# Hybrid decoder trunk: side work issued ahead of the weight parts in each half chunk, four output columns by turns, and a later rope stage

## The chip, the cores and the metric

One Trainium2 chip, one of its cores. The metric is the device time of one execution in microseconds (us). Three runs of the kernel before gave 1641.02, 1641.28 and 1642.7 us; the median is 1641.28 us.

## What is computed

Two layers over a sequence of 256 tokens of width 1024, batch 1, all in float32. Cut to what matters:

```
for l in range(2):
    x = x + 0.5 * swiglu(rms_norm(x, ffn1_norm[l]), ffn1_w_gu[l], ffn1_w_down[l])
    h = rms_norm(x, mix_norm[l])
    z = h @ w_in[l]           # q_a, k_a, v_a, q_b, f_b, i_b, og_b, gate_a, gate_b
    y_a = dilated_attention(rope(q_a), rope(k_a), v_a) @ w_att_branch[l]     # 3 groups, 4 heads
    o_b = rms_norm(hgrn2_recurrence(q_b, f_b, i_b, lb[l]), hgrn_head_norm[l])  # 8 heads
    y_b = (o_b * silu(og_b)) @ w_hgrn_branch[l]
    x = x + (sigmoid(gate_a) * y_a + sigmoid(gate_b) * y_b) @ w_mix_out[l]
    x = x + cross_attention(rms_norm(x, xattn_norm[l]), rms_norm(mem, mem_norm[l]),
                            xattn_wq[l], xattn_wkv[l], xattn_wo[l])          # 4 heads of 256
    x = x + 0.5 * swiglu(rms_norm(x, ffn2_norm[l]), ffn2_w_gu[l], ffn2_w_down[l])
return rms_norm(x, final_norm)
```

## The kernel before, in words

**Weights.** All weights come through one stream of 4288 blocks of 128 x 128, in the order in which they are used. A chunk is 16 blocks (1 MB, one DMA on the SyncE queue, three buffers `raw`), a half chunk is 8. For precision every weight is split in two: `whi` is the block rounded to the matmul's type (a cast on ScalarE, L104, 128 x 1024 elements for a half chunk), `wlo` is the rest (a subtraction on VectorE, L110). Activations are split in the same way, high part by ScalarE (L277 or L287), low part by VectorE (L280 or L288). One block is two matmuls: L323 multiplies `whi` with both parts of the activation (512 columns), L324 multiplies `wlo` with the high part (256 columns). Where the tokens are the output's rows (`tm`), it is L297 to L299.

**The stream's clock.** `take` hands out blocks. At the first block of half chunk i it calls `prep(i + 3, i + 2)`, which issues `whi` for half chunk i + 3 and `wlo` for i + 2 (five and four buffers), and the load of the chunk two further on. Then it calls `on_half`, which is `tick`. `tick` runs what was deferred to this half chunk and takes one step of one piece of side work. All engines execute in the order of issue.

**Side work.** `defer(n, f)` runs f n half chunks later. `side(generator, period)` adds a generator; each `yield` ends a step. Side work is the norm statistics (`Norm.steps`; of the memory once, with `keep="mem"`, after `mem_stats` has added its squares, L374 on ScalarE and L376 on VectorE, between the half chunks of the first feed-forward), the rope tables and bounds (`setup`), the recurrence (`hgrn`: steps of matmuls L645 and VectorE work L651 to L661; its output matmuls are L692 and L694) and one attention generator per head (`attention`: scores L739 and L743, softmax, transposes L765 to L768, value products L777 and L779).

**A group of matmuls.** `fm` takes a pair buffer of PSUM (there are three; `bank` has two) and multiplies two columns of weights, 16 blocks for an inner size of 1024. The `evac` that it is given runs behind the last matmul. In most stages that is `add_halves`: ScalarE copies one half (L344), and half a chunk later VectorE adds the other (L347), after which the stage's own work follows: in the feed-forward L510 (times the norm), L511 (Silu on ScalarE), and a half chunk later L518 and the split L277 and L280; in the mixer's merged gate L917, L919, L277 and L280. `fm_beside` does the same for four columns by turns in two pair buffers, and runs both `evac`s at the end.

**Residual updates.** `mm_resid` runs an output product column pair by column pair; `Resid.take` then adds both halves to x (L434 on VectorE, twice), forms the next operand's parts (L287 on ScalarE, L288 on VectorE) and adds squares for the next norm (L374 and L376). None of this is deferred.

**The mixer's order** is written out: eight recurrence groups, then values, output gates and gates by turns with the twelve `query_key` groups (three to a head). In `query_key`, `stage1` (half a chunk after the group's end) copies halves on ScalarE (L878, L879) and multiplies on GpSimd (L880); `stage2`, one half chunk later, does L884 and L885 on VectorE; one half chunk after the last group's `stage2` the head's attention begins. What is left then runs in `drain`. Next come the merged gate (eight groups of 12 blocks) and the output product `w_mix_out`.

**In the cross-attention** each head's product of probabilities and values (L293 to L295) goes to a `bank`, and is split by L277 and L280.

Of the kernel before, what the change touches and what calls it, by code (L numbers as in the profile page):

```python
# [12 lines left out]
OP = mybir.AluOpType  # L13
# [4 lines left out]
D = 1024  # L18
P = 128
# [27 lines left out]
class Stream:  # L47
# [65 lines left out]
    def take(self, descs):  # L113

        n = len(self.order)
        i, o = divmod(n, HALF)
        assert o + len(descs) <= HALF
        self.order.extend(descs)
        if o == 0:
            self.prep(i + 3, i + 2)  # L120
            self.on_half()
            self.hi.pop(i - 1, None)
            self.lo.pop(i - 1, None)
        s = slice(o * P, (o + len(descs)) * P)
        return self.hi[i][:, s], self.lo[i][:, s]


def build(tc, a, nchunks):
# [237 lines left out]
    class Norm:  # L366
# [25 lines left out]
        def steps(self, keep=None):  # L392
            st = bank()
            for i in range(2):
                nc.tensor.matmul(st[:, i:i + 1], self.acc[:, i * P:(i + 1) * P], ones[:, :1],
                                 start=True, stop=True)
            ms = tiny.tile([P, 2], F32, name="ms")
            nc.vector.tensor_scalar(ms, st[:, :2], 1.0 / D, EPS, op0=OP.mult, op1=OP.add)
            pool = tiny if keep is None else consts
            self.r = pool.tile([P, 2], F32, name="rstd" + (keep or ""))  # L400
            nc.gpsimd.tensor_tensor(self.r, ms, mhalf[:, :2], op=OP.pow)
            dg = tmp()
            for i in range(2):
                nc.vector.tensor_scalar(dg[:, i * P:(i + 1) * P], ident, self.r[:, i:i + 1], None, op0=OP.mult)
            yield
            yield
            b = bank()
            nc.tensor.matmul(b[:, :T], ones, dg, start=True, stop=True)
            self.bc = (tiny if keep is None else consts).tile([P, T], F32, name="bc" + (keep or ""))
            nc.scalar.copy(self.bc, b[:, :T])  # L410
# [29 lines left out]
    class Last:  # L440
# [32 lines left out]
        def finish(self, g):  # L473
            st = pair()
            for i in range(2):
                s = slice(i * P, (i + 1) * P)
                nc.tensor.matmul(st[:, i:i + 1], self.acc[:, s], ones[:, :1], start=True, stop=False)
                nc.tensor.matmul(st[:, i:i + 1], self.sq[:, s], ones[:, :1], start=False, stop=True)
            ms = tiny.tile([P, 2], F32, name="ms")
            r = tiny.tile([P, 2], F32, name="rstd")  # L480
            nc.vector.tensor_scalar(ms, st[:, :2], 1.0 / D, EPS, op0=OP.mult, op1=OP.add)
            nc.gpsimd.tensor_tensor(r, ms, mhalf[:, :2], op=OP.pow)
            self.turn(KD - 1, g)
            for i in range(2):
                o, y = self.o[i], a["y"][i * P:(i + 1) * P]
                nc.vector.tensor_scalar(o[:, :512], o[:, :512], r[:, i:i + 1], None, op0=OP.mult)
                nc.scalar.activation(o[:, 512:], self.b[i], AF.Copy, scale=r[:, i:i + 1])
                nc.sync.dma_start(y[:, :512], o[:, :512])
                (nc.sync, nc.scalar)[i].dma_start(y[:, 512:], o[:, 512:])

    def mm_resid(name, l, act, K, res):
        n = 2 if K == KD else 1
        for j in range(0, KD, n):
            fm([(name, l, (j + i) * P, act, K) for i in range(n)],
               lambda left, right, j=j: res.take(j, left, right))

# [238 lines left out]
    def attention(l, h, qk, v, out):  # L735
# [21 lines left out]
        nc.vector.tensor_scalar(s0[:, :384], s0[:, :384], den[:, 0:1], None, op0=OP.mult)  # L757
        nc.vector.tensor_scalar(s1[:, :768], s1[:, :768], den[:, 1:2], None, op0=OP.mult)
        yield
        yield  # L760
        b0, b1 = bank(), pair()
        p0, p1 = slot(), slot()
        for g in range(NG):
# [26 lines left out]
    def mixer(l, res, nxt):  # L790
# [76 lines left out]
        def query_key(u):  # L867
            hd, g = divmod(u, NG)
            if g == 0:
                qks[hd] = Row()  # L870
            row = qks[hd]

            def evac(left, right):
                d, t = row.two(2 * g), join()
                r = two(t)

                def stage1():
                    nc.scalar.copy(r[:64], d[64:])  # L878
                    nc.scalar.copy(r[64:], d[:64])  # L879
                    nc.gpsimd.tensor_tensor(r, r, both(sb), op=OP.mult)  # L880
                    defer(1, stage2)

                def stage2():
                    nc.vector.tensor_tensor(d, d, both(cb), op=OP.mult)  # L884
                    nc.vector.tensor_tensor(d, d, r, op=OP.add)  # L885
                    if g == NG - 1:
                        qk = [(row(2 * i), row(2 * i + 1)) for i in range(NG)]
                        defer(1, lambda: side(attention(l, hd, qk, v, aout), 2))
                add_halves(d, left, right, stage1)
            c = g * 512 + hd * P  # L890
            fm([("w_in", l, CQ + c, h, KD), ("w_in", l, CK + c, h, KD)], evac)
# [29 lines left out]
                add_halves(two(t), left, right, stage1, last)  # L921
            fm([("w_att_branch", l, j * P, aout, AH), ("w_hgrn_branch", l, j * P, hout, HH)], evac)
        r = nxt()
        mm_resid("w_mix_out", l, mg, KD, r)
        return r


# [33 lines left out]
    def xattn(l, res, hm, nxt):  # L961
# [30 lines left out]
        drain()  # L992
        o = Act()
        for hd in range(XH):
            b = bank()
            for d in range(2):
                o0 = (2 * (hd % 2) + d) * P
                for c in range(2):
# [114 lines left out]
```

## Time and profile before

| | |
|---|---|
| median of three runs | 1641.28 us |
| lowest and highest | 1641.02 and 1642.7 us |
| the profiled execution's own time | 1640.77 us |
| its span (first to last instruction) | 1639.0 us |
| mean granted clock of TensorE | 0.998 |
| instructions | 26419 |
| HBM read | 286.18 MB |

The span is the time between the first and the last instruction that the profiler saw; 1.77 us lie around it. PE is TensorE's matmuls and PEld its weight loads, DVE is VectorE, ACT ScalarE, POOL GpSimd, SP SyncE. Matmuls are pipelined and their ends are modelled: TensorE is called busy in time in which a matmul is only drawn out, so waits on it are read from starts as well. In a row, the bracket at the end is the engine's idle time before the instruction and what ended it. L numbers are lines of the kernel.

### The profile page before, as it was taken

The numbers are of one execution on the slowest core, as the hardware profiler recorded it, in microseconds if no ns is written. First come the engines' busy times: TensorE is split into PE (matmuls) and PEld (weight loads), VectorE is DVE, ScalarE is ACT, GpSimd is POOL, SyncE is SP. The second block draws the span as 40 slices with busy tenths as digits, with TensorE's granted clock in tenths as the row PEclk, the third lists the DMA queues.
The fourth block names the chain that finished last, engine by engine and source line by source line (L and its number), as shares of the span: only waits on it lengthen the run. The fifth ranks groups of instructions, "written<-read, shape, count | busy, mean of one in ns | idle before, by whom it ended". The sixth has DMA issues, their size and how long they took to land.

```text
span 1639.0 us, 26419 instructions
## 1 busy us (share of the span) xinstructions
PE 1618.5 (99%) x10818; PEld 1414.8 (86%) x10818; DVE 1240.8 (76%) x1804; ACT 925.7 (56%) x1381; POOL 63.0 (4%) x46
## 2 busy tenths in 40 slices
PE   9999999999999999999999999999999999999998
PEld 7888888888888888888888888888888888888887
DVE  7887687767868868877677776777788787688764
ACT  6665454656565656655456655546565656466542
POOL 0000000102100000000000000001111000000000
PEclk9999999999999999999999999999999999999999
DMA  8555554434445534555555564544334454355552
GB/s 303 183 181 211 199 182 180 155 130 154 154 154 180 197 137 171 190 190 196 184 185 197 182 223 176 191 172 150 144 133 159 174 180 179 129 206 180 193 191 79
DMA packets 41593, 288.94 MB, mean 176 GB/s; under 512 B 4864, under 2 KB 4992, under 8 KB 7424
## 3 DMA queue, kind: packets, MB, share of 16 engines
q1 hardware_dynamic: 41040, 286.67, 49.0%
q8 instruction: 85, 1.39, 0.3%
q10 hardware_dynamic: 432, 0.59, 0.1%
q14 instruction: 36, 0.29, 0.1%
HBM read 286.18 MB, written 1.05 MB: 175 GB/s over the span
## 4 chain that ended last, share of the span: by engine, by line
PE 90%; DVE 6%; ACT 2%; issue 1%; DMA 0%; POOLq 0%; POOL 0%; ACTq 0%; DVEq 0%
PE pair L323 49%; PE pair L324 25%; PE pair L297 3%; PE pair L298 3%; PE pair L299 3%; DVE wlo L110 2%; PE bank L645 1%; DVE join L347 1%; DVE slot L280 1%; PE bank L777 1%; PE pair L336 1%; DVE join L917 1%; PE pair L743 0%; PE bank L293 0%; PE bank L294 0%
## 5 line engine op out<-in xcount | busy, mean ns | idle before, releaser
L323 PE MATMUL pair<-slot,whi 128*128 128x512 f32 x3808 | 1337.4, 395 | 4.8 <-DVE slot L280 2.5
L324 PE MATMUL pair<-slot,wlo 128*128 128x256 f32 x3808 | 1065.9, 280 | 0.0
L323 PEld LDWEIGHTS pair<-slot,whi 128*128 128x128 f32 x3808 | 713.4, 187 | 167.4 <-DVE slot L347 3.1
L324 PEld LDWEIGHTS pair<-slot,wlo 128*128 128x128 f32 x3808 | 719.2, 189 | 0.6
L110 DVE TENSOR_TENSOR wlo<-raw,whi 128x1024 fp32r<-128x1024 f32 x532 | 640.1, 1221 | 43.2 <-ACT whi L104 42.9
L104 ACT CAST whi<-raw 128x1024 fp32r<-128x1024 f32 x532 | 546.7, 1046 | 15.5 <-PE pair L299 6.1
L344 ACT COPY join<-pair 128x512 f32<-128x512 f32 x136 | 79.6, 586 | 181.8 <-PE pair L324 181.7
L347 DVE TENSOR_TENSOR join<-pair,join 128x512 f32<-128x512 f32 x136 | 93.7, 690 | 107.1 <-ACT join L344 107.0
L287 ACT ACTIVATE slot<-x,vecs 128x256 fp32r<-128x256 f32 x64 | 30.9, 506 | 133.2 <-DVE x L434 132.0
L297 PE MATMUL pair<-whi,slot 128*128 128x512 f32 x224 | 89.2, 398 | 0.0
L299 PE MATMUL pair<-whi,slot 128*128 128x512 f32 x224 | 87.4, 390 | 0.0
L298 PE MATMUL pair<-wlo,slot 128*128 128x512 f32 x224 | 87.4, 390 | 0.0
L344 ACT COPY slot<-pair 128x512 f32<-128x512 f32 x48 | 28.1, 586 | 102.7 <-PE pair L324 102.7
L277 ACT CAST slot<-join 128x256 fp32r<-128x256 f32 (+1 forms) x120 | 51.7, 435 | 50.8 <-DVE join L919 26.0
L434 DVE SCALAR_TENSOR_TENSOR x<-pair,x 128x256 f32<-128x256 f32 (+1 forms) x80 | 42.5, 531 | 49.2 <-PE pair L324 47.7
L511 ACT ACTIVATE tmp<-join 128x256 f32<-128x256 f32 x88 | 36.4, 417 | 52.5 <-DVE join L510 52.4
L510 DVE TENSOR_TENSOR join<-join,bc 128x512 f32<-128x512 f32 x88 | 60.5, 692 | 5.1 <-ACT bc L410 2.4
L880 POOL TENSOR_TENSOR join<-join,sinb 128x512 f32<-128x512 f32 x24 | 42.1, 1753 | 421.7 <-ACT join L879 392.8
L280 DVE TENSOR_TENSOR slot<-join,slot 128x256 fp32r<-128x256 f32 (+1 forms) x120 | 54.0, 455 | 2.8 <-ACT slot L277 2.8
L347 DVE TENSOR_TENSOR slot<-pair,slot 128x512 f32<-128x512 f32 x48 | 33.1, 689 | 27.5 <-ACT slot L344 27.4
L288 DVE SCALAR_TENSOR_TENSOR slot<-x,vecs,slot 128x256 fp32r<-128x256 f32 x64 | 29.6, 484 | 27.0 <-ACT slot L287 27.0
L299 PEld LDWEIGHTS pair<-whi,slot 128*128 128x128 f32 x224 | 42.0, 188 | 9.0
(184 smaller groups left out, 1029.9 us busy)
## 6 DMA issues: line engine op xcount, KB each, us to landing
raw<-w SPq DMA_DIRECT2D x266, 1024.0 KB, 4.8
slot<-mem SPq DMA_DIRECT2D x6, 512.0 KB, 6.7
raw<-w SPq DMA_DIRECT2D x3, 512.0 KB, 7.8
y<-slot SPq DMA_DIRECT2D x3, 256.0 KB, 2.3
cst<-cst SPq DMA_DIRECT2D x1, 721.0 KB, 10.2
x<-x SPq DMA_DIRECT2D x2, 256.0 KB, 4.3
x<-x SPq DMA_DIRECT2D x1, 512.0 KB, 7.0
raw<-w ACTq DMA_DIRECT2D x1, 256.0 KB, 5.1
```

What stands on the lines that cost most here:

```text
L104: nc.scalar.copy(self.hi[i], r)
L110: nc.vector.tensor_tensor(self.lo[i], r, self.hi[i].bitcast(F32), op=OP.subtract)
L277: nc.scalar.copy(h, src)
L280: nc.vector.tensor_tensor(l, src, h.bitcast(F32), op=OP.subtract)
L297: nc.tensor.matmul(out, ah, wh, start=first, stop=False)
L298: nc.tensor.matmul(out, ah, wl, start=False, stop=False)
L299: nc.tensor.matmul(out, al, wh, start=False, stop=last)
L323: nc.tensor.matmul(whole[:, i * 512:(i + 1) * 512], wh, act.parts(k), start=k == 0, stop=False)
L324: nc.tensor.matmul(whole[:, i * 512:i * 512 + T], wl, act.hi(k), start=False, stop=k == K - 1)
L344: nc.scalar.copy(d, right)
L347: nc.vector.tensor_tensor(d, left, d, op=OP.add)
L510: nc.vector.tensor_tensor(two(t), two(t), both(n.bc), op=OP.mult)
```

## The change

It has six parts. In `take`, `on_half` comes ahead of `prep` (but for the very first half chunk). The memory's norm yields once more ahead of its second matmul. The last norm's four matmuls are put in another order and two PSUM banks. The mixer's output product does its first four columns by turns, with both residual updates at the end. In the mixer, rope's second stage and the attention behind it come two half chunks later instead of one, each, and the attention yields once less after its softmax. In the cross-attention, heads 2 and 3 use pair buffers.

```
 def take(self, descs):
         if o == 0:
+            if i == 0:
+                self.prep(i + 3, i + 2)
+            self.on_half()
             self.prep(i + 3, i + 2)
-            self.on_half()
...
 Norm.steps:
             yield
             yield
+            if keep:
+                yield
             b = bank()
...
 Last.finish:
             for i in range(2):
-                s = slice(i * P, (i + 1) * P)
-                nc.tensor.matmul(st[:, i:i + 1], self.acc[:, s], ones[:, :1], start=True, stop=False)
-                nc.tensor.matmul(st[:, i:i + 1], self.sq[:, s], ones[:, :1], start=False, stop=True)
+                nc.tensor.matmul(st[:, i * 512:i * 512 + 1], self.acc[:, i * P:(i + 1) * P], ones[:, :1],
+                                 start=True, stop=False)
+            for i in range(2):
+                nc.tensor.matmul(st[:, i * 512:i * 512 + 1], self.sq[:, i * P:(i + 1) * P], ones[:, :1],
+                                 start=False, stop=True)
...
-    def mm_resid(name, l, act, K, res):
+    def mm_resid(name, l, act, K, res, turns=False):
         n = 2 if K == KD else 1
-        for j in range(0, KD, n):
+        first = 0
+        if turns:
+            first = 4
+            fm_beside([(name, l, j * P, act, K) for j in range(4)],
+                      [lambda left, right, j=j: res.take(j, left, right) for j in (0, 2)])
+        for j in range(first, KD, n):
...
 attention, after the softmax:
         yield
-        yield
         b0, b1 = bank(), pair()
...
 query_key, stage1 and stage2:
-                    defer(1, stage2)
+                    defer(2, stage2)
...
-                        defer(1, lambda: side(attention(l, hd, qk, v, aout), 2))
+                        defer(2, lambda: side(attention(l, hd, qk, v, aout), 2))
...
 mixer:
-        mm_resid("w_mix_out", l, mg, KD, r)
+        mm_resid("w_mix_out", l, mg, KD, r, True)
...
 xattn:
         for hd in range(XH):
-            b = bank()
+            b = bank() if hd < 2 else pair()[:, :512]
```

## Rows read from the trace of the kernel before

**Rows 1.** The page: busy time of each engine with its share of the span and its instructions, and the loads of weight chunks (number, KB each, median us from issue to landing).
```profile
PE 1618.5 (99%) x10818; PEld 1414.8 (86%) x10818; DVE 1240.8 (76%) x1804; ACT 925.7 (56%) x1381; POOL 63.0 (4%) x46
...
raw<-w SPq DMA_DIRECT2D x266, 1024.0 KB, 4.8
```
**Rows 2.** Busy time by window, of the L323 matmuls alone (one to a block), in a stretch of the first feed-forward. Columns: window, its length, PE busy (instructions), PEld busy (instructions), granted clock, DMA share, GB/s.
```profile
43.96:99.43 55.47, 55.47 (x161) 29.81 (x160) 1.00 0.50 177
```
**Rows 3.** The waits of TensorE's matmuls: engine and line, whom it waited for, us in total, times, longest.
```profile
PE pair L323 <- DVE slot L280: 2.5, 2, 1.6
PE pair L323 <- DVE slot L347: 2.3, 2, 1.2
PE bank L293 <- DVE slot L280: 1.6, 2, 0.8
PE bank L739 <- DVE slot L885: 1.5, 2, 0.8
...
PE bank L408 <- DVE tmp L404: 1.0, 1, 1.0
```
**Rows 4.** The timeline of TensorE in the mixer of layer 0: start, us from the first start to the last end, engine, line, operation, names, shapes, number of instructions merged, idle time before.
```profile
266.48 0.39 PE L298 MATMUL pair<-wlo,slot 128*128 128x512 f32 x1
...
303.67 0.60 PE L739 MATMUL bank<-slot 128*128 128x128 f32 x4
305.03 0.49 PE L739 MATMUL bank<-slot 128*128 128x128 f32 x2 [0.75 <-DVE slot L885]
...
361.03 0.83 PE L739 MATMUL bank<-slot 128*128 128x128 f32 x6
361.69 1.46 PE L743 MATMUL pair<-slot 128*128 128x256 f32 x6
362.80 0.58 PE L323 MATMUL pair<-slot,whi 128*128 128x512 f32 x1
...
406.45 1.46 PE L743 MATMUL pair<-slot 128*128 128x256 f32 x6
...
409.08 0.50 PE L323 MATMUL pair<-slot,whi 128*128 128x512 f32 x1 [1.17 <-DVE slot L347]
...
488.29 0.40 PE L323 MATMUL pair<-slot,whi 128*128 128x512 f32 x1
```
**Rows 5.** The groups of instructions of the whole span: the subtraction that makes `wlo` and the cast that makes `whi` (busy us, mean ns of one, idle time of the engine before them and what ended it).
```profile
L110 DVE TENSOR_TENSOR wlo<-raw,whi 128x1024 fp32r<-128x1024 f32 x532 | 640.1, 1221 | 43.2 <-ACT whi L104 42.9
L104 ACT CAST whi<-raw 128x1024 fp32r<-128x1024 f32 x532 | 546.7, 1046 | 15.5 <-PE pair L299 6.1 <-ACT whi L104 3.6 <-DVE wlo L110 1.7
```
**Rows 6.** The timeline of VectorE over most of one cycle of two half chunks in the first feed-forward of layer 0.
```profile
79.36 0.69 DVE L347 TENSOR_TENSOR join<-pair,join 128x512 f32<-128x512 f32 x1
80.08 0.69 DVE L510 TENSOR_TENSOR join<-join,bc 128x512 f32<-128x512 f32 x1
81.56 0.42 DVE L376 TENSOR_TENSOR tmp<-tmp 128x256 f32<-128x256 f32 x1 [0.79 <-ACT tmp L374]
81.91 1.22 DVE L110 TENSOR_TENSOR wlo<-raw,whi 128x1024 fp32r<-128x1024 f32 x1
83.04 0.42 DVE L518 TENSOR_TENSOR join<-tmp,join 128x256 f32<-128x256 f32 x1
```
**Rows 7.** The timeline of ScalarE in the same cycle.
```profile
77.44 0.59 ACT L344 COPY join<-pair 128x512 f32<-128x512 f32 x1
...
83.49 0.41 ACT L277 CAST slot<-join 128x256 fp32r<-128x256 f32 x1 [1.02 <-DVE join L518]
83.92 1.28 ACT L547 ACT_TABLE_LOAD   x1
```
**Rows 8.** The timeline of VectorE at the recurrence's first step with L645 in layer 0.
```profile
256.20 2.36 DVE L110 TENSOR_TENSOR wlo<-raw,whi 128x1024 fp32r<-128x1024 f32 x2 [3.23 <-ACT whi L104]
260.16 0.69 DVE L347 TENSOR_TENSOR slot<-pair,slot 128x512 f32<-128x512 f32 x1 [1.60 <-ACT slot L344]
...
265.49 0.43 DVE L661 COPY_PREDICATED tmp<-cpm,bank 128x128 f32<-128x128 uint32 x1
```
**Rows 9.** The timeline of ScalarE and VectorE at the start of the merged gate in layer 0.
```profile
481.62 0.58 ACT L344 COPY join<-pair 128x512 f32<-128x512 f32 x1
...
483.07 0.69 DVE L347 TENSOR_TENSOR join<-pair,join 128x512 f32<-128x512 f32 x1
...
484.52 0.42 DVE L919 TENSOR_TENSOR join<-join 128x256 f32<-128x256 f32 x1
...
484.98 0.41 ACT L277 CAST slot<-join 128x256 fp32r<-128x256 f32 x1 [1.84 <-DVE join L919]
```
**Rows 10.** The timeline of VectorE in the mixer's output product of layer 0: the residual updates of the first and the second column pair, and the `wlo` that follow each.
```profile
515.08 1.42 DVE L434 SCALAR_TENSOR_TENSOR x<-pair,x 128x512 f32<-128x512 f32 x2 [0.69 <-PE pair L324]
...
518.43 2.35 DVE L110 TENSOR_TENSOR wlo<-raw,whi 128x1024 fp32r<-128x1024 f32 x2
...
520.73 1.42 DVE L434 SCALAR_TENSOR_TENSOR x<-pair,x 128x512 f32<-128x512 f32 x2
...
524.39 1.22 DVE L110 TENSOR_TENSOR wlo<-raw,whi 128x1024 fp32r<-128x1024 f32 x1
```
**Rows 11.** Busy time by window around a wait of TensorE in layer 1's output product: window, length, PE, PEld, DVE, ACT and POOL busy (instructions), granted clock, DMA share, GB/s.
```profile
1319.00:1323.00 4.00, 2.39 (x14) 1.85 (x13) 3.13 (x5) 2.30 (x3) 0.00 (x0) 1.00 0.00 0
```

More of the change, by code (lines that the diff above doesn't have):

```diff
@@ L475, in finish @@
             for i in range(2):
-                s = slice(i * P, (i + 1) * P)
-                nc.tensor.matmul(st[:, i:i + 1], self.acc[:, s], ones[:, :1], start=True, stop=False)
-                nc.tensor.matmul(st[:, i:i + 1], self.sq[:, s], ones[:, :1], start=False, stop=True)
+                nc.tensor.matmul(st[:, i * 512:i * 512 + 1], self.acc[:, i * P:(i + 1) * P], ones[:, :1],
[3 more added lines that the diff above has]
+                                 start=False, stop=True)
             ms = tiny.tile([P, 2], F32, name="ms")
             r = tiny.tile([P, 2], F32, name="rstd")
-            nc.vector.tensor_scalar(ms, st[:, :2], 1.0 / D, EPS, op0=OP.mult, op1=OP.add)
+            nc.vector.tensor_scalar(ms, two(st)[:, :, 0], 1.0 / D, EPS, op0=OP.mult, op1=OP.add)
             nc.gpsimd.tensor_tensor(r, ms, mhalf[:, :2], op=OP.pow)
```

## The prediction

> **What bounds the kernel now.** I read the page first, then the list of waits on TensorE, then the timeline of TensorE around each wait, and last the timelines of VectorE and ScalarE in four places. The page shows TensorE busy for nearly the whole span [rows 1]. In a feed-forward stretch of 55.47 us there are 161 blocks (one L323 matmul each), 0.3445 us a block, 2.77 us a half chunk [rows 2]. So time can only be won where TensorE stands still, and it is lost wherever TensorE comes to stand still. The list of waits has five entries that this diff touches, 8.9 us together [rows 3]; matmul ends are modelled, so the starts say more. The six L739 take 1.85 us from 303.67 against 0.83 us at 361.03; from the first L743 to the next L323 it is 2.63 us at 406.45 against 1.11 us at 361.69 [rows 4]. So one wait costs 1.0 and 1.5 us where the idle column says 0.75 and 1.17, some 0.2 to 0.3 more.
>
> **What the change takes away**, each at both layers unless said:
> - Rope's second stage a half chunk later, attention two: L885 is then long done when L739 comes. 2 x 1.0 = 2.0 us.
> - With that, a head's scores no longer fall into the half chunk behind the recurrence's output matmuls, which hold one of three pair buffers. At 406.45 the scores took the free one, and L323 waited for L347 to empty the last. 2 x 1.5 = 3.0 us.
> - Heads 2 and 3 of the cross-attention in pair buffers: the L293 wait, 1.6 us idle [rows 3], at 0.16 more each, 1.9 us. The new buffers are handed back long before, so nothing is late next; bounds 1.6 and 2.0.
> - One more yield ahead of the memory norm's L408: 1.1 us, once.
> - Two pairs by turns in the output product: channel 6 of the merged gate is needed 24 blocks after the start, not 12. The L323 wait on L280, 2.5 us idle in two places [rows 3], is 2.8 us by starts.
> - The order of the four last matmuls: 0.1 us.
>
> Sum 10.9 us. The yield taken out of the attention balances its later start: the transposes and the value product fall in the half chunks where they fell. DMA: a chunk's load is now issued behind the side work's own loads and after a later wlo, but four half chunks, 11 us, ahead of its first cast, and lands in 4.8 us [rows 1]; I cost it at nothing, and some us at one place if it came 6 us late.
>
> **What it adds.** TensorE's order is the same. What moves is L104 (1.05 us) and L110 (1.22 us) [rows 5], 532 of each, behind the side work on queues that go on only when their head can. Two waits thereby cover less: wlo for two half chunks on must now wait until the side work in front has had its own wait, and an ACT copy L344 at the end of a group stands behind a cast that used to be ahead.
>
> *Ordinary feed-forward.* Side work L347, L510, then wlo: L344 + L347 + L510 + wlo = 0.6 + 1.4 + 1.2, ready 3.4 us into a window of 5.5. Cost nothing; DVE's slack is the cover.
>
> *First feed-forward, layer 0*, where the memory's squares are added in seven of the pairs of half chunks. Today's cycle on DVE, and on ACT beside it: [rows 6, 7]. Behind one another in the new order stand, start to start, L344 to L347 0.62, to L510 0.72, to L376 1.48 (it waits 0.79 for ACT), to wlo 0.35, to L518 1.13, to L277 0.45, to the cast 0.31, to the next L344 0.95. That is 6.0 us against 5.54, so 0.47 lost in each of seven, 3.3 us. The table load of 1.28 us at 83.92 [rows 7], its way back and two sines are in the same ACT chain, and I put 2.0 us on them (less than two loads, since one partly falls into a wait). The first wlo is ready 4.6 us into 5.8, so 1.2 us is cover. 3.3 + 2.0 - 1.2 = 4.1, taken as 4.0 us; bounds 0 and 7.
>
> *First step of the recurrence* [rows 8]: wlo ran at 256.20 with DVE then idle until 260.16; now it comes behind L347 and the step, which keep DVE until 265.9. It would end at 267.07, and L298 wants it at 266.48 [rows 4]. 0.6 us, twice: 1.2 us. Later steps end earlier against their need; nothing.
>
> *Merged gate* [rows 9]: after the sigmoids ACT is behind. L344 at 481.62, L347 to L919 1.9 us, L277, then the cast (now between), L344, again 1.9 us, wlo 1.2: 481.6 + 0.6 + 1.9 + 0.4 + 1.0 + 0.6 + 1.9 + 1.2 = 489.2; neighbours overlap by 0.2 in all, so 489.0, and L324 wants this wlo 0.23 us after 488.29 [rows 4]. 0.5 us, twice: 1.0 us. The same sum carried through the eight groups keeps pace with TensorE but never catches up: the last group's L344 stands behind a cast until 510.9, and the wlo behind that group's work, for the third half chunk of the output product, comes at 515.8, 1.2 us too late.
>
> *Output product.* Today each pair's residual update keeps DVE from 515.08 to 518.43 (first) or 520.73 to 524.39 [rows 10], 3.4 and 3.7 us, and the two starts, 5.65 us apart, are the pace of 16 blocks. With four columns by turns two updates come at once: 0.2 + 3.4 + 3.7 + 1.2 for the wlo behind them = 8.5 us, and TensorE wants that wlo 5.65 + 0.23 us after the group's end. 2.6 us. Before, DVE sits idle, since wlo for that half chunk is issued after the updates. The next two updates have 0.3 us too little. Per layer 1.2 + 2.6 + 0.3 = 4.1, twice: 8.2 us; bounds 0 and 10. So this part gives 2.8 and costs 8.2.
>
> **The sum.** 4.0 + 1.2 + 1.0 + 8.2 = 14.4 added, 10.9 taken away: 3.5 us more. The profiled execution took 1640.77 us (span 1639.0), 0.5 below the median 1641.28. 1641.28 + 3.5 = 1644.8 us.
>
> **A rule weighed.** The granted clock is 1.00, its upper level of 2.4 GHz, from 1319 to 1323 us [rows 11], across the longest of the L323 waits on L280, 1.6 us idle [rows 3]; the new ones are up to 2.6 us. The Trainium skill (TensorE: Matmul & The Clock Gate, HAM oscillation — how this bites in real kernels) says that a gap of idle TensorE, if long enough, returns its clock to the half rate, 1.2 GHz. By it the time would be that of rival 3; the trace has no gap of this size.
>
> **Rivals.**
> 1. *The casts don't bind* (faster). In the first feed-forward and the merged gate the new order is absorbed: ACT is idle nearly half of the span, and DVE waited only 43 us for casts [rows 5]. Price 4.0 + 1.0 + 2.4 = 7.4: 1637.4 us. It decides where the cycle of 6.0 us really stays under 5.54, which it does if the square or the L277 cast is half a microsecond sooner. Against it: today's rows follow the program's order without exception, with DVE full in that stretch. 0.26.
> 2. *Everything is covered*, the two updates too, and all 10.9 us arrive: 1630.4 us. 0.06; the 8.5 us against 5.9 speak against it.
> 3. *The clock falls* after the wait in each output product, and a half chunk runs at half rate: 2 x 2.8 more, 1650.4 us. 0.06.
> 4. *The change doesn't do what it says at the pair buffers*: the group behind the recurrence takes the buffer that L347 is still to empty, now behind L884 and L885. Instead of 3.0 won, 2 x 3 lost: 1653.8 us. At 406.45 the longest-free buffer was taken, which speaks against it. 0.06.
>
> **Chances and range.** The forecast has 0.56, its own range is 1641 to 1649. About 0.2%, 3.3 us, is what a measurement tells from no change, so of the 0.56 some 0.36 is slower and 0.20 the same. Rival 1 gives 0.22 faster and 0.04 the same, rival 2 0.06 faster, 3 and 4 slower 0.12. Faster 0.28, same 0.24, slower 0.48. The range 1633 to 1651 leaves out rivals 2 and 4 and some tails, and covers the bounds of the first feed-forward and most of those of the output product.
>
> **What would show it.** Right: no wait left at L739, L408 and L293; L324 waiting for wlo L110 (no such wait is in the list today), some 2.6 us in the first half chunk after the two updates of each output product, 0.6 us in the first step of the recurrence, and several us between 78 and 100 us; VectorE's L347 waiting longer for L344. Wrong: L324 never waits for wlo; then the time goes to 1637 or below. If the wait in the output product is there but none in the first feed-forward, step "first feed-forward" failed and the time is near 1641.

## The result and the profile after

The changed kernel took 1646.97 us, the median of six runs from 1644.65 to 1648.55, against 1641.15 us for the kernel before in the same series: a ratio of 1.0037 (95% interval 1.0024 to 1.0050), so 5.8 us slower. A second series gave 1645.15 us and 1.0029 (1.0018 to 1.0039). The execution profiled below took 1648.55 us, the longest of its six, and one step below shows why that matters.

The page of the changed kernel: its span, the busy time of each engine, and the loads of weight chunks (compare [rows 1]).
```profile
span 1646.8 us, 26215 instructions
...
PE 1624.9 (99%) x10818; PEld 1415.4 (86%) x10818; DVE 1242.6 (75%) x1804; ACT 924.7 (56%) x1381; POOL 64.6 (4%) x46
...
raw<-w SPq DMA_DIRECT2D x266, 1024.0 KB, 4.8
```
Each engine has as many instructions as before (the total also counts semaphore instructions, which keep no engine busy), and the loads land as fast as they did. Yet TensorE is "busy" 6.4 us longer with the same 10818 matmuls. A wait adds little to busy time: of the longest one below, 2.24 us from start to start where 0.23 is usual, 1.85 us are idle. So part of the loss must lie in slower matmuls.

The waits of TensorE's matmuls in the changed kernel (engine and line, whom it waited for, us in total, times, longest), against [rows 3]. The file has grown: L323 and L324 are now L325 and L326, L298 is L300, L344 and L347 are L346 and L349, L434 is L438; L338 and L339 are the matmuls of four columns by turns, which the output product now uses too.
```profile
PE pair L326 <- DVE wlo L110: 7.2, 8, 1.8
...
PE pair L339 <- DVE wlo L110: 2.2, 2, 1.2
...
PE pair L300 <- DVE wlo L110: 0.7, 2, 0.4
```
All five entries of [rows 3] are gone. In their place stands one kind of wait that the kernel before did not have: TensorE waits for a `wlo` of L110, 10.1 us in 12 places. VectorE's L349 waits 121.8 us for the copy L346, against 107.0 us in the kernel before.

VectorE in the output product of layer 0, to be laid beside [rows 10] (start, us from first start to last end, engine, line, operation, names and shapes, number merged, idle time before):
```profile
521.75 1.42 DVE L438 SCALAR_TENSOR_TENSOR x<-pair,x 128x512 f32<-128x512 f32 x2 [1.59 <-PE pair L339]
523.75 0.89 DVE L290 SCALAR_TENSOR_TENSOR slot<-x,vecs,slot 128x256 fp32r<-128x256 f32 x2 [0.58 <-ACT slot L289]
524.76 0.43 DVE L378 TENSOR_TENSOR tmp<-tmp 128x256 f32<-128x256 f32 x1
525.10 1.41 DVE L438 SCALAR_TENSOR_TENSOR x<-pair,x 128x512 f32<-128x512 f32 x2
...
528.75 2.35 DVE L110 TENSOR_TENSOR wlo<-raw,whi 128x1024 fp32r<-128x1024 f32 x2
```
Two updates in a row hold VectorE for 7.0 us (521.75 to 528.75), and only then come two `wlo` back to back. TensorE in the same place:
```profile
527.79 0.39 PE L325 MATMUL pair<-slot,whi 128*128 128x512 f32 x1
530.03 0.46 PE L326 MATMUL pair<-slot,wlo 128*128 128x256 f32 x1 [1.85 <-DVE wlo L110]
530.29 0.63 PE L325 MATMUL pair<-slot,whi 128*128 128x512 f32 x1
530.72 0.41 PE L326 MATMUL pair<-slot,wlo 128*128 128x256 f32 x1
530.93 0.63 PE L325 MATMUL pair<-slot,whi 128*128 128x512 f32 x1
```
After the wait the matmuls themselves are longer: a pair that took 0.35 us now takes 0.64, from start to start. Busy time by window of the changed kernel behind this wait in both layers (window, length, PE, PEld, DVE, ACT, POOL busy and instructions, granted clock, DMA share, GB/s; compare [rows 11]):
```profile
527.00:535.00 8.00, 6.15 (x27) 5.10 (x26) 7.09 (x13) 5.49 (x12) 0.00 (x0) 0.79 0.34 120
1339.00:1347.00 8.00, 6.16 (x27) 5.09 (x26) 7.18 (x12) 5.49 (x10) 0.00 (x0) 0.79 0.35 133
```
27 matmuls in 8 us of which 1.85 are idle, at a mean granted clock of 0.79: part of the window ran at the lower level of 1.2 GHz.

### The profile page after: what moved, and what is told of

It is laid out like the page before. It is cut to its first block, busy times and chain, and to the rows that moved or that the text cites. A ratio compares the mean times of both kernels' runs of the same rounds, so it can differ in the third digit from the quotient of the medians.

```text
span 1646.8 us, 26215 instructions
## 1 busy us (share of the span) xinstructions
PE 1624.9 (99%) x10818; PEld 1415.4 (86%) x10818; DVE 1242.6 (75%) x1804; ACT 924.7 (56%) x1381; POOL 64.6 (4%) x46
## 3 DMA queue, kind: packets, MB, share of 16 engines
q8 instruction: 85, 1.39, 0.3%
## 4 chain that ended last, share of the span: by engine, by line
PE 90%; DVE 5%; ACT 4%; issue 1%; DMA 0%; POOLq 0%; ACTq 0%; DVEq 0%
PE pair L325 48%; PE pair L326 25%; PE pair L299 3%; PE pair L300 3%; PE pair L301 3%; ACT whi L104 2%; PE bank L656 1%; DVE wlo L110 1%; DVE join L349 1%; PE pair L338 1%; DVE join L927 1%; PE pair L754 1%; PE bank L787 1%; ACT join L346 1%; PE pair L339 1%
## 5 line engine op out<-in xcount | busy, mean ns | idle before, releaser
L325 PE MATMUL pair<-slot,whi 128*128 128x512 f32 x3744 | 1321.5, 397 | 0.0
L326 PE MATMUL pair<-slot,wlo 128*128 128x256 f32 x3744 | 1049.1, 280 | 7.2 <-DVE wlo L110 7.2
L325 PEld LDWEIGHTS pair<-slot,whi 128*128 128x128 f32 x3744 | 703.6, 188 | 162.2 <-DVE slot L282 0.4
L326 PEld LDWEIGHTS pair<-slot,wlo 128*128 128x128 f32 x3744 | 707.9, 189 | 10.9 <-DVE wlo L110 9.8
L110 DVE TENSOR_TENSOR wlo<-raw,whi 128x1024 fp32r<-128x1024 f32 x532 | 641.1, 1224 | 27.9 <-ACT whi L104 27.1
L104 ACT CAST whi<-raw 128x1024 fp32r<-128x1024 f32 x532 | 540.0, 1045 | 13.7 <-issue 5.6
L349 DVE TENSOR_TENSOR join<-pair,join 128x512 f32<-128x512 f32 x136 | 93.9, 691 | 122.1 <-ACT join L346 121.8
L346 ACT COPY join<-pair 128x512 f32<-128x512 f32 x136 | 79.3, 584 | 98.4 <-PE pair L326 98.3
L300 PE MATMUL pair<-wlo,slot 128*128 128x512 f32 x224 | 87.6, 391 | 0.7 <-DVE wlo L110 0.7
L438 DVE SCALAR_TENSOR_TENSOR x<-pair,x 128x256 f32<-128x256 f32 (+1 forms) x80 | 42.4, 530 | 54.4 <-PE pair L326 49.6
L346 ACT COPY slot<-pair 128x512 f32<-128x512 f32 x48 | 28.1, 585 | 78.9 <-PE pair L326 78.9
L349 DVE TENSOR_TENSOR slot<-pair,slot 128x512 f32<-128x512 f32 x48 | 33.1, 689 | 40.7 <-ACT slot L346 40.7
L300 PEld LDWEIGHTS pair<-wlo,slot 128*128 128x128 f32 x224 | 42.1, 188 | 9.6 <-DVE wlo L110 1.6
```

The costliest lines, as they stand in the source:

```text
L104: nc.scalar.copy(self.hi[i], r)
L110: nc.vector.tensor_tensor(self.lo[i], r, self.hi[i].bitcast(F32), op=OP.subtract)
L300: nc.tensor.matmul(out, ah, wl, start=False, stop=False)
L325: nc.tensor.matmul(whole[:, i * 512:(i + 1) * 512], wh, act.parts(k), start=k == 0, stop=False)
L326: nc.tensor.matmul(whole[:, i * 512:i * 512 + T], wl, act.hi(k), start=False, stop=k == K - 1)
L346: nc.scalar.copy(d, right)
```

## The experiments

Eleven runs, each against the kernel before on the same chip. To place each gain, I compare the time between the starts of two half chunks in one trace with the same time in the kernel before; the load at the start of the kernel, whose length differed by up to 2.2 us from profile to profile, then cancels. In us against the kernel before, by half chunk numbers, both layers added where a part has two:
```
stretch (half chunks)       after  after  e1     e2     e3     e4     e5     e9     e10
                                   again  old    no     neither order cast   gate   no
                                          order  turns         only  ahead  cast   exp
first feed-forward, 24-32   +3.98  +3.98   0.00  +3.99   0.00  +3.97 +2.62  +3.98  +2.58
memory norm, 32-36          -1.33  -1.22  -1.18  -1.28  -1.18  -1.23 -1.33  -1.29  -1.24
first step, 88-92, 358-362  +1.26  +1.42   0.00  +1.43   0.00  +1.37 +1.38  +1.24  +1.46
rope, 100-150, 362-418      -5.69  -5.26  -5.98  -5.67  -5.98  +1.47 -5.96  -5.30  -5.26
gate, 150-162, 418-430      +1.98  +2.03  +0.01  +1.99   0.00  +2.05 +0.49  +0.48  +1.99
output, 162-172, 430-440    +6.71  +5.36  +1.68  +1.06  +0.32  +1.07 +1.78  +1.67  +6.58
cross-att., 176-194,444-462 -2.09  -2.10  -2.11  -2.07  -2.11  +0.05 -2.11  -2.09  -2.09
46-70, 214-270, 270-340     +3.21  +0.03  -0.10  +3.19  -0.10  +3.19 +2.13  +2.15  +1.09
```
The last line holds the first three of the four down products of the feed-forwards. All these numbers are of one profiled execution of each kernel.

**e1_old_order**: the changed kernel with the old order in `take`.
```
-            if i == 0:
-                self.prep(i + 3, i + 2)
-            self.on_half()
             self.prep(i + 3, i + 2)
+            self.on_half()
```


> The changed kernel with the old order in take (weights' parts first, then side work); all its other parts stay. Theory (the new order costs time of its own, and the four columns by turns cost more than they save): the waits of L326 on wlo in the first feed-forward (3.5 us), at the recurrence's first step (2 x 0.6) and in the merged gate (2 x 0.6) are gone, the 2 us wait in each output product and the lower clock behind it stay. Against the kernel before: -1.3 (memory norm) - 5.7 (rope and pair buffers) - 2.1 (cross-attention) + 2 x 3.3 (output product) = 2.5 us faster, about 1638.7 us. Rival A (the order is harmless, only the turns cost): no faster than the changed kernel by more than a microsecond, about 1646. Rival B (most of the loss is the slower pace of the matmuls, 2.83 against 2.77 us a half chunk, that the changed kernel shows in three of four down products): about 3 us above the first number unless the pace returns with the order.


Measured: 1632.5 us, ratio 0.9954 (0.9940 to 0.9967). 6 us less than expected, and by the table nearly all of it (4.9) in the output product: +1.7 where I had left +6.6. The wait in its third half chunk and, in the profiled execution, the fall of the clock went with the new order.

**e2_no_turns**: the new order stays, `mm_resid` goes without turns.
```
-        mm_resid("w_mix_out", l, mg, KD, r, True)
+        mm_resid("w_mix_out", l, mg, KD, r)
```


> The changed kernel without the four columns by turns (column pairs one after another as before); its new order and its other parts stay. Theory: the wait of some 2 us behind the two residual updates goes, the half rate of the clock behind it too, and L325's wait on L282 in the second half chunk comes back at about 1.8 us. Per layer 3.9 us less than the changed kernel, about 1639 us. Rival A (the turns cost, the order is harmless): the same number, but then no wait of L326 on wlo in the first feed-forward. Rival C (the turns save what they were meant to): slower than the changed kernel, about 1650 us.


Measured: 1641.28 us, ratio 1.0003 (0.9994 to 1.0012). Close to no change, 2 us over the expectation.

**e3_neither**: both edits above; the later rope stage, the pair buffers of the cross-attention and the norm's yield stay.


> The changed kernel with the old order in take and without the turns: what is left is the later rope stage and attention, the memory norm's yield, the pair buffers in the cross-attention and the last norm's order. Theory: -1.3 - 5.7 - 2.1 - 0.1 = 9.2 us less than the kernel before, about 1632 us; waits left on TensorE: L325 on L282 in the output product, 2.5 us, and no L326 on wlo. Rival A (the order is harmless): as without turns alone, about 1639. Rival B (slower pace comes with the later rope stage or the buffers): about 1635.


Measured: 1631.28 us, ratio 0.9944 (0.9931 to 0.9956). Its waits on TensorE:
```profile
PE pair L323 <- DVE slot L280: 2.5, 2, 1.6
```
Of the waits of [rows 3] only the one that the turns are for is back. So the small parts bring 9.5 us alone.

**e4_order_only**: the kernel before with the order of the changed one.


> The kernel before with one edit: on_half ahead of prep. Theory: +3.5 in the first feed-forward, +1.3 at the recurrence's first step, +1.5 a layer in the merged gate and output product (the copy L344 now stands behind a cast), -1.0 a layer at L739 and -1.1 a layer at the pair buffer (side work has no 1.1 us subtraction ahead of it): about 3.6 us slower than the kernel before, 1644.8 us. Rival A (the order is harmless or a gain, since it lets side work finish sooner): 1637 to 1641 us, with no L324 wait on wlo.


Measured: 1650.69 us, ratio 1.0067 (1.0054 to 1.0080): the order alone costs 9.9 us, not the 4 I expected. Its waits on TensorE:
```profile
PE pair L326 <- DVE wlo L110: 5.2, 8, 1.7
PE pair L325 <- ACT whi L104: 3.2, 2, 1.6
PE pair L325 <- DVE slot L349: 2.0, 2, 1.0
PE bank L741 <- DVE slot L887: 1.5, 2, 0.7
```
The last two are the waits at the pair buffer and at the scores [rows 3], of which the expectation had the order win 2.2 and 2.0 us. They are still there, and the rope stage is 1.5 us longer instead of 4.2 shorter; the 3.2 us of the down products stood nowhere in the expectation.

e2 against e3 says the same with the other parts in place: 1641.28 - 1631.28 = 10.0 us. With the turns it is 1646.97 - 1632.5 = 14.5 us, and the turns cost 5.7 us in the new order and 1.2 in the old (12.7, 3.9 and 1.2 with the changed kernel's second series, 1645.15). The two edits do each other harm.

In the traces so far three down products ran at 2.827 us a half chunk wherever the order was new (the expectations say 2.830), and at 2.773 wherever it was old. The next two kernels ask which half of the swap does what.

**e5_cast_ahead**: the changed kernel, with the cast alone put back ahead.
```
+            self.prep(i + 3, -1)
...
             self.on_half()
             self.prep(i + 3, i + 2)
```


> The changed kernel (1647.0 us) with one half of the swap undone: ScalarE's cast whi of three half chunks on is issued ahead of the side work again, VectorE's wlo stays behind it. My theory (the first feed-forward and the merged gate lose time because the cast and the wlo stand in one chain of ScalarE and VectorE behind the side work): taking the cast out of the chain brings the cycle of the first feed-forward from 6.0 to about 5.0 us, under the 5.5 of TensorE, so its 3.9 us go, and 1.0 at the gates and 2.4 at the third half chunk of the output product with them; the recurrence (1.2) and the wait behind the two updates stay: 1639.7 us. Rival, the wlo on VectorE alone costs: 1645 to 1647 us. The half chunks of the down products (2.830 us in every kernel with the new order so far, 2.773 in every one with the old) stay at 2.830 if the wlo's place sets them; if the cast's place does, 3.2 us less, 1636.5.


Measured: 1639.21 us, ratio 0.9994 (0.9985 to 1.0003). The total agrees to 0.5 us, the places do not. In the first feed-forward only 1.4 of 4.0 us came back, and 1.7 of the 2.6 that stay lie in one half chunk, behind the second table load; the third half chunk of the output product (2.5 us) and the gates (1.5) came back about as foreseen; the rest is a clock that did not fall in the profiled execution (below), 2.4 us, and one down product that ran at 2.773, 1.1.

**e6_low_ahead**: the changed kernel, with `wlo` alone put back ahead.
```
+            self.prep(i + 2, i + 2)
...
             self.on_half()
             self.prep(i + 3, i + 2)
```


> The changed kernel (1647.0 us) with the other half of the swap undone: VectorE's wlo of two half chunks on is issued ahead of the side work again, ScalarE's cast stays behind it. My theory: the chain of the first feed-forward is cut as well, since wlo then needs only a cast of the half chunk before (3.9 us back), the recurrence's 1.3 and the gates' 1.0 and 2.4 go too, and the wait behind the two updates of the output product falls to what the old order had with turns, about 2 us per layer, without the fall of the clock: 1634 to 1636 us at half chunks of 2.830 us in the down products, 1632 at 2.773. Rival, the cast's place on ScalarE alone costs: 1642 us or more. Both rivals wrong and both halves back to 1633 would mean that only the two together cost.


Measured: 1832.54 us, ratio 1.1166 (1.1150 to 1.1181). That is 186 us more than the changed kernel: my theory was plainly wrong here. Waits in the whole kernel:
```profile
DVE wlo L110 <- ACT whi L104: 353.1, 232, 3.4
...
ACT tmp L523 <- DVE join L522: 190.9, 81, 2.8
...
PE pair L327 <- DVE wlo L110: 75.0, 84, 3.6
```
`wlo` now stands at the head of VectorE's queue before its cast is made; the cast stands on ScalarE behind side work, which waits for VectorE's side work, which is queued behind that `wlo`. In the old order, where `wlo` also comes first, the cast has a whole half chunk of lead, and VectorE waited only 42.9 us for it [rows 5].

**e7_turns_early**: the changed kernel, with the casts and `wlo` of the next half chunk issued ahead of the two updates.
```
...
+        if early:
+            i = len(W.order) // HALF
+            W.prep(i + 3, i + 2)
         for whole, evac in zip(wholes, evacs):
```


> The changed kernel (1647.0 us), with the casts and wlo for the next half chunk issued ahead of the two residual updates of the first four columns of the output product, not behind them; nothing else differs. My theory: the wait of 2.0 us behind the two updates goes in both layers, and the half rate behind it (some 1.6 us a layer) with it: 2 x 3.6 = 7.2 us less, 1639.8 us. Rival 1, the fall of the clock has another cause (the stretch ahead of it, with its wait of 1.2 us): 4.0 us less, 1643 us, granted clock still under 0.8 in a few us there. Rival 2, the updates now end 1.2 us later and the next pair of groups waits for them: no more than 2 us less, 1645 us.


Measured: 1643.48 us, ratio 1.0017 (1.0007 to 1.0026). 3.5 us less than the changed kernel, rival 1's number, but by another way: the fall of the clock is gone (granted 1.00 there), while the wait is not; it came two half chunks later.
```profile
534.56 0.39 PE L326 MATMUL pair<-slot,wlo 128*128 128x256 f32 x1 [0.86 <-DVE wlo L110]
```
Four updates of about 3.5 us [rows 10] and eight `wlo` of 1.22 us [rows 5] are some 24 us of VectorE's time in eight half chunks of 2.83 us, 22.6 us of TensorE's. Moving one of them only moves the place where it runs out.

**e8_best**: the same in the old order (e1 with the early `prep`).


> The old order of casts and side work, all other parts of the change, the two pairs by turns among them, and the casts for the next half chunk issued ahead of the two updates. The same without that last step took 1632.5 us, with one wait for wlo of 1.9 us (2.0 by starts) in each output product. My theory: these two go: 1628.5 us, 2.8 us under the kernel without turns (1631.3). Rival: the turns give nothing in the old order, since the updates are late instead: 1631 to 1633 us.


Measured: 1630.84 us, ratio 0.9939 (0.9926 to 0.9951), the lowest of all, 1.7 us under e1, but level with e3 (1631.28). The rival holds: even so the turns give about nothing. Its wait has moved two half chunks on too:
```profile
PE pair L324 <- DVE wlo L110: 1.7, 2, 0.9
```

**e9_gate_cast**: the changed kernel with the cast ahead only in the merged gate and the first half chunks of the output product.
```
+            if 150 <= i <= 164 or 418 <= i <= 432:
+                self.prep(i + 3, -1)
             self.on_half()
             self.prep(i + 3, i + 2)
```


> The changed kernel (1647.0 us), but in the half chunks of the merged gate and in the first three of the output product (both layers) ScalarE's cast is issued ahead of the side work again; everywhere else the new order stays. Theory A (the granted clock falls behind the wait of 2.2 us after the two updates only where a wait of 1.4 to 1.5 us came some 12 us ahead of it): the waits in the third half chunk go (2 x 1.2 us), the wait behind the two updates stays at 2.1 to 2.2 us, and the granted clock stays at 1.00 behind it, 2 x 1.6 us; with up to 1 us at the gates, 1640.4 to 1641.4 us. Theory B (the wait of 2.2 us alone brings the clock down): 1643.6 to 1644.6 us, granted clock under 0.8 behind it as in the changed kernel.


Measured: 1641.35 us, ratio 1.0002 (0.9993 to 1.0011), the number of theory A; as a rule the theory does not stand, as the part on the clock shows. TensorE no longer waits in the third half chunk, the wait behind the two updates is as long as before, and the clock stays up. Busy time by window, e9 (columns as above):
```profile
525.00:533.00 8.00, 6.16 (x36) 5.13 (x34) 7.18 (x12) 5.48 (x10) 0.00 (x0) 1.00 0.36 131
1333.00:1341.00 8.00, 6.29 (x35) 5.03 (x33) 7.18 (x13) 5.48 (x9) 0.00 (x0) 1.00 0.37 133
```
The same 6.2 us busy out of 8, and 36 matmuls where the changed kernel did 27.

**e10_no_exp**: the changed kernel without the table loads of the first feed-forward (and without the exponential that needs them, so that the recurrence works with other bounds).
```
-        nc.scalar.activation(e, e, AF.Exp)
+        nc.scalar.copy(e, e)
```


> The changed kernel (1647.0 us) with a plain copy in place of the exponential of the recurrence's lower bounds (16 columns; the gates of the recurrence are then other values), so that ScalarE loads no other table in the first feed-forward and none to come back: two loads of 1.28 us less. My prediction put 2.0 us on the loads and 2.1 us on the chain of ScalarE and VectorE. If that split holds, the waits between 76 and 100 us fall from 3.9 to about 2 us, the one of 1.85 us behind 89.3 us above all: 1645.0 us. Rival, the chain alone makes the waits and the loads fall into ScalarE's slack: 1646.5 to 1647 us. Rival 2, the loads start it all: no wait over 0.2 us is left there, 1643 us.


Measured: 1642.3 us, ratio 1.0010 (1.0001 to 1.0019). In the stretch concerned +2.58 us are left of +3.98: the loads cost 1.4 us, the chain 2.6. The wait at 89.31 us in the changed kernel (2.08 us from start to start) is 0.73 us here; first the changed kernel, then e10:
```profile
89.31 0.39 PE L325 MATMUL pair<-slot,whi 128*128 128x512 f32 x1
91.39 0.39 PE L326 MATMUL pair<-slot,wlo 128*128 128x256 f32 x1 [1.69 <-DVE wlo L110]
```
```profile
88.93 0.39 PE L325 MATMUL pair<-slot,whi 128*128 128x512 f32 x1
89.66 0.39 PE L326 MATMUL pair<-slot,wlo 128*128 128x256 f32 x1 [0.34 <-DVE wlo L110]
```
The total fell by more than that (3 to 5 us); two of its three down products ran at 2.773 in the profiled execution, which is 2.1 us of it. That execution took 1645.44 us, one of the two slowest of eleven, and the clock fell in both layers; the other nine (1640.78 to 1643.1 us) have a higher mean granted clock, as the part on the clock tells, so its median has less of the fall than its trace.

**e11_after_again**: the changed kernel, unaltered.


> The changed kernel once more, unaltered, for a second profile of it. If the length of a half chunk (2.773 or 2.830 us for a whole stage) is set by the program, the down products of both feed-forwards of layer 0 and of the first one of layer 1 run at 2.830 us again, the first products of the cross-attention at 2.773, and the clock falls to under 0.8 behind the same two waits; if it differs from execution to execution, at least one of these stages changes over. Time 1645 to 1648.5 us.


Measured: 1645.15 us (1643.44 to 1647.31), ratio 1.0029 (1.0018 to 1.0039). Its profiled execution has a span of 1641.7 us, 5.1 less than the first profile of the same program. A window over the first down product of layer 0, TensorE's matmuls into pair buffers (window, length, PE busy and instructions, granted clock, DMA share, GB/s), first in the first profile, then in e11, then in e1:
```profile
150.00:205.46 55.46, 55.26 (x313) 1.00 0.52 189
```
```profile
150.00:205.46 55.46, 55.26 (x319) 1.00 0.53 195
```
```profile
150.00:205.46 55.46, 55.26 (x320) 1.00 0.50 181
```
No idle time (the last 0.2 us are other matmuls), granted clock 1.00 in all, and yet 2% fewer matmuls in the first: 2.827 us a half chunk against 2.773. And behind the wait after the two updates, in e11, layer 0 and layer 1:
```profile
526.00:534.00 8.00, 6.15 (x27) 5.03 (x26) 7.18 (x13) 5.48 (x10) 0.00 (x0) 0.79 0.38 131
1335.00:1343.00 8.00, 6.16 (x35) 5.18 (x35) 7.18 (x13) 5.49 (x11) 0.00 (x0) 1.00 0.37 131
```
The clock fell in one layer and not in the other. Neither the pace nor the fall is thus fixed by the program: they differ between executions.

## Why the prediction held, and where it did not

The direction and the main cause held: TensorE lost some 13 us to the new waits for `wlo` (4.0 + 1.3 + 1.3 + 2.5 + 4.0, below) against 12.3 that the change took away. That the size is near, 3.5 us forecast and 5.8 and 4.3 measured in the two series, is partly luck. Point by point:

- **What it takes away**: 10.9 us forecast. Measured: memory norm 1.2 (1.1 forecast); rope and pair buffers 6.0 in e1 and e3 (5.0); cross-attention 2.1 (1.9). The wait on L280 went, in e1 as in the changed kernel: 1.1 and 1.9 us by starts in the first half of the output product (2.8 for both). Together 12.3: a little more than the sum had. The 0.1 us for the order of the last four matmuls can't be read: from the start of the last half chunk to the end it took 11.82 us before and 11.57 to 11.92 with the new order. Rival 4 (the pair buffer still to be emptied) did not occur. One term is not the edit's alone: in e4 the order by itself takes away the L408 wait.
- **First feed-forward**: 4.0 forecast, 3.97 to 3.99 in six traces with the new order (the changed kernel twice, e2, e4, e7, e9). ScalarE's L346 starts at 86.96 and 92.96, the cycle of 6.0 us that I summed up. The split was off: 2.0 for table loads and 2.1 for the chain were 1.4 and 2.6 (e10). And the reason that I gave in e5's expectation, that the cast alone makes the chain too long, failed: with the cast ahead 2.6 us remain.
- **Recurrence**: 1.2 forecast, 1.3 and 1.4 measured; TensorE waits at L300, as said. **Merged gate**: 1.0 forecast; the half chunk with the wait is 0.65 us longer in each layer. The stage lost 2.0 us, of which 0.6 is the slow pace of layer 1's gate, that [rows 4] could not show.
- **Output product, third half chunk**: 1.2 us a layer forecast, 1.16 and 1.32 measured (1.39 and 1.55 from start to start, less the usual 0.23).
- **Output product, behind the two updates**: 2.6 + 0.3 a layer forecast, 2.0 measured (2.24 from start to start). The 0.3 shows only where the clock stayed up: there half chunks 170 and 438, right behind the product, are 0.3 to 0.4 us longer (e11's layer 1, e1, e5, e9); in the changed kernel's first profile they are not. The first update starts at 521.75, half a microsecond ahead of the next group's first matmul (522.25), since columns 0 and 1 are complete before 2 and 3; I had let it start 0.2 behind. But the clock fell behind it, which I had only as rival 3 with a chance of 0.06. It cost some 1.3 us a time, net of that 0.3 to 0.4, not a whole half chunk of 2.8: layer 1's product from half chunk 434 to 440 grew by 3.73 us in the first profile, with the fall, and by 2.41 in e11, without.
- **What the sum lacked**: the pace of the down products, 3.2 us in the first profile, none in e11.
- **Slips in the working** that change no term: the window of [rows 2] holds 160 blocks and the edge of one more, so a block takes 0.3467 us, which gives the 2.77 a half chunk that the prediction goes on with (eight times 0.3445 would be 2.76); and the ordinary feed-forward's 0.6 + 1.4 + 1.2 is 3.2, not 3.4.

With these the first profile closes: 4.0 + 1.3 + 2.0 + 9.7 (output product: 6.7 net of the 3.0 won) + 3.2 = 20.2 added, 12.3 taken away, 7.9 us; the two profiled executions are 7.8 apart (1648.55 and 1640.77). Without the fall (2.6) and the pace (3.2) it would be +2.1, and each of the two comes in some executions only; that fits medians of +4 to +6. So the forecast of +3.5 is near for a reason that is partly luck: the terms that it had came to 1.4 us less than it said, and two that it lacked add up to 5.8.

**The clock.** The trace of before shows a clock of 1.00 across a wait of 1.6 us [rows 3, 11], and I gave the fall a small chance. In the profiled executions a wait of 2.1 to 2.2 us (from start to start, as all waits in this part) lost the clock in five of six cases where another of 1.4 to 1.5 us had come 12.4 us earlier (the changed kernel, e10 and e11), and in none of six where that first wait was missing (e1, e5, e9). e9's profile lost the first wait alone, and with it the fall. That is theory A, and two things on record speak against it as a rule.

The first is e6. There the clock fell behind a single wait of 2.11 us, ahead of which TensorE had been busy without a break for 18 us. Busy time by window before the wait, the wait itself, and busy time by window behind it:
```profile
450.00:468.00 18.00, 18.00 (x109) 16.00 (x108) 13.90 (x19) 9.89 (x15) 1.27 (x1) 1.00 0.38 137
```
```profile
470.85 0.27 PE L777 MATMUL pair<-cst,slot 128*128 128x128 f32 x1
472.96 0.86 PE L779 MATMUL bank<-cst,slot 128*128 128x128 f32 x3 [1.84 <-DVE tmp L731]
```
```profile
473.00:476.40 3.40, 3.40 (x12) 3.01 (x13) 1.31 (x3) 3.38 (x8) 1.29 (x1) 0.50 0.08 34
```
The same wait in layer 1 of e6 (at 1373.82, as long) kept the clock, and so did one of 2.24 us at 1479.23, 12.9 us after one of 1.95, and in each layer's cross-attention three of 2.11, 2.35 and 2.64 us, 9 to 10 us apart. Over all thirteen traces, between the first half chunk and the kernel's end, 6 of 29 waits of 2.0 to 2.7 us lost the clock, and 4 of 4 of 3.9 us (all in e6); one more fall came with three shorter waits within 5 us (0.93, 1.26 and 1.62, at 555.39 in e6).

The second is the mean granted clock of the executions that were not profiled. One fall of 3.4 us takes 0.001 off it: the nine traces here without a fall have 0.998 or 0.999, those with a fall in both layers (the changed kernel, e10) 0.997 and 0.996. By my estimate from these traces an execution at 0.997 or less had at least one fall, though not where. Without the first wait that is 5 of 11 executions of e5 (its five slowest, 1640.47 to 1641.38 us, against 1638.71 to 1639.21), 1 of 5 of e1 and none of 11 of e9; with it, 6 of 14 of the changed kernel and 2 of 11 of e10 (1645.44 and 1645.87 us, the first of which is the profiled one, against 1640.78 to 1643.1). Among the kernels without a wait of 2.1 us in the output product (the kernel before, e2, e3, e4, e7, e8) no execution on record is that low.

So what the runs show is that a wait of some 2 us can bring the clock down, that it does so in some executions of a kernel and not in others, and that a first wait is neither needed nor enough. Whether it makes a fall likelier, and what decides, stays open. The Trainium skill (TensorE: Matmul & The Clock Gate, HAM oscillation — how this bites in real kernels) has one gap of idle TensorE, if it is long enough, return the clock to the half rate. The runs agree that idle TensorE does it, as behind all four waits of 3.9 us; between 2.0 and 2.7 us one gap's length alone does not tell: 2.24 us kept the clock in e1, e5 and e6 and lost it in the changed kernel and e11, and 2.64 us kept it in e6.

**The pace.** That the new order sets the down products' pace, as the first traces suggested, fell with e11. In sum, of the three stages in the four profiles with the old order (the kernel before, e1, e3, e8) 12 of 12 ran at 2.773; in the eight with the new one, or half of it (the changed kernel twice, e2, e4, e5, e7, e9, e10; e6 is left out, since its stages wait), 8 of 24. So in these stages the slow pace came with the new order only, if not always, worth about 2 us on average (16 of 24 stages at 1.07 us). Elsewhere the old order has it too: the kernel before runs layer 0's merged gate at 2.827 us a half chunk, and e8 both layers'. Every matmul there is a little late, with no wait recorded; by what, no run here shows. It stays open.

**The order alone** cost 10 us where I expected 4 of e4, which had it win 4.2 us at the scores and the pair buffer; it won nothing there. By the table, e2 against e3: 4.0 in the first feed-forward, 1.4 in the recurrence, 2.0 at the gates, 0.7 in the output product, 0.3 in the rope stage and 3.3 in the down products, 11.7 us in the two profiles; the medians are 10.0 apart, and e2's profiled execution was the slowest of its eleven.

## What to carry to other kernels

When producers of operands share queues with side work, move neither behind the other without summing the queue's time up to the consumer's need, in each stage by itself: here one swap on two queues cost 10 us and hid a gain of 9.5 us from the small edits beside it. A producer of two steps on two engines (cast, then subtract) needs its lead between the steps more than its place in either queue; e6 lost some 186 us by that. Bundling two evacuations so as to lengthen the time to the next need pays only if the engine that evacuates has time left in that stage: count its work against the matmuls' before trying (24 us against 22.6 here).

## What the runs showed of the hardware

- A wait of TensorE of 2.0 to 2.7 us from start to start brought its granted clock down to 0.50 for 3.4 us in 6 of 29 cases, and one of 3.9 us in 4 of 4. At 2.2 us it differs between executions of one program, and within one: in e11 the clock fell in layer 0 and not in layer 1.
- The mean granted clock of an execution, which every run has, tells of such falls where no trace was taken: it stood at 0.998 or 0.999 in the traces without one and at 0.996 and 0.997 in those with two.
- TensorE, with no wait and a granted clock of 1.00, held one of two steady paces for a whole stage: a half chunk of 2.773 or 2.827 us, 2% apart (matmul pairs start 346.7 or 353.3 ns apart). The same program took the one in one execution and the other in another, and the difference over three stages is 3.2 us, more than half of what the change cost.
- The spans of two profiles of the same program lay 5.1 us of 1640 apart (1646.8 and 1641.7 us): 3.2 are the pace, 1.3 the fall of the clock in one layer, 1.1 the load at the start. Each wait repeated to 0.2 us. Waits can be read from one trace; the pace of a stage and the clock want a second.
